# Gates and mix_out of a decoder layer in pairs of column blocks, with seven block products for half of the depth, and the head's later loads moved behind its splits

## The chip, the core and the metric

The kernel runs on one core of one Trainium2 chip. The metric is the device time of one execution in microseconds (us). Most executions of one kernel agree within 0.3%.

## The reference

One decoder layer on 256 tokens of width 2048, all in float32. What matters here:

```python
h = rms_norm(x, norm_mix)
q, k, v, cx, cb, cc, ga, gc = split_in_proj(h @ w_in)
...
y_attn = merge_heads(moba_attention(q, k, heads(v, N_ATTN_HEADS))) @ w_attn_out
y_conv = (cb * short_conv(cc * cx, conv_w)) @ w_conv_out
merged = jax.nn.sigmoid(ga) * y_attn + jax.nn.sigmoid(gc) * y_conv
x = x + merged @ w_mix_out
hq = heads(rms_norm(x, norm_xattn) @ wq_x, N_XATTN_HEADS)
mk, mv = jnp.split(rms_norm(mem, norm_mem) @ wkv_x, 2, axis=-1)
...
u = jax.nn.relu(rms_norm(x, norm_mlp) @ w_up)
return x + (u * u) @ w_down
```

`w_in` is 2048 x 10240: 1024 columns each for q, k, v, cx, cb and cc, and 2048 each for the two gates ga and gc. `w_attn_out` and `w_conv_out` are 1024 x 2048, `w_mix_out` 2048 x 2048, `w_up` 2048 x 8192, `w_down` 8192 x 2048.

## The kernel before, in words

**Products.** A float32 operand is written as the sum of a high and a low part of type float32r, and a product is three matmuls: high by high, high by low, low by high (L103 to L105). TensorE (PE) multiplies a stationary 128x128 piece of the activations by 128 rows x 512 columns of the weights and adds into a PSUM bank.

**Weights.** They are streamed from HBM in raw tiles of 128x2x512 (two blocks of 128 rows, 512 KB) by SP's DMA queue (`load_w`, L58). ScalarE (ACT) rounds a tile to its high part (`whi`, L66), VectorE (DVE) subtracts to get the low part (`wlo`, L67); each is one instruction of 128x1024. The pool of raw tiles has 6 buffers, the pool of split ones 5 of each kind.

**Column groups.** `tok_group` (L107) makes 512 output columns for all 256 tokens: two PSUM banks, one for each 128 tokens, and for each block of 128 rows three matmuls of 512 columns a bank. A group 2048 deep is 96 matmuls and eight weight tiles. `feat_group`, used for w_up, gives the output transposed.

**Stages, in order of the program.** The head: w_in's first 512 columns, while x's features are still being loaded (`xf` into `xraw`, with the weights, on SP's queue) and split (`split_scaled`, L134/L135). x by tokens (`xtok`, 2 MB in four DMAs on ACT's queue, L246) is loaded in the same stretch, and its sums of squares (L189) are made on ACT; from them comes r1, the RMS factor that is multiplied in when a group is taken out of PSUM (L204). Then q, k, v; attention; the convolution's three groups and its elementwise part `y` (L318 to L321); then the loop over four column blocks j (L329): two groups of w_in for the gates with the sigmoid read from PSUM on ACT (L333), attn_out (L337), conv_out (L341, L342) and eight transposes that turn the merged block into features (`mg`). Then `residual` for mix_out: four groups, each added to xtok (L355) and transposed into `x2g` (L134/L135), with `memory(j)` after each: a load of mem by features (L372, ACT's queue) into a buffer of the pool `blk` (3 buffers), split into `memT`, and a load of mem by tokens (L376) for its sums of squares. Then cross attention and the MLP.

**Order.** The Tile framework places each engine's instructions by its own timeline, so they stand in another order than the program writes them; each engine and queue then runs its own list in order. Where an instruction needs a buffer, it waits until the buffer's last reader is done.

## Time and profile before

| what | value |
|---|---|
| median of 3 runs | 1476.53 us (1476.36 to 1476.88) |
| the profiled execution: its own time | 1476.77 us |
| its span, first to last instruction | 1475.0 us |
| mean granted TensorE clock | 0.996 of full speed |
| PE busy | 1454.8 us, 99% of the span |
| DVE busy | 820.9 us, 56% |
| ACT busy | 691.2 us, 47% |
| DMA | 281.27 MB, 191 GB/s on average |

Busy times are sums over instructions of the time between the start and the end that the profiler gives; on DVE and ACT an instruction that waits for nothing can start before the end of the one before it. The profile's 40 slices show PE at 9 tenths or more in all but the first slice (6). The execution's own time is 1.8 us more than its span, for what lies before the first and after the last instruction.

### The profile page before, as it was taken

The numbers are of one execution on the slowest core, as the hardware profiler recorded it, in microseconds if no ns is written. First come the engines' busy times: TensorE is split into PE (matmuls) and PEld (weight loads), VectorE is DVE, ScalarE is ACT, GpSimd is POOL, SyncE is SP. The second block draws the span as 40 slices with busy tenths as digits, with TensorE's granted clock in tenths as the row PEclk, the third lists the DMA queues.
The fourth block names the chain that finished last, engine by engine and source line by source line (L and its number), as shares of the span: only waits on it lengthen the run. The fifth ranks groups of instructions, "written<-read, shape, count | busy, mean of one in ns | idle before, by whom it ended". The sixth has DMA issues, their size and how long they took to land.

```text
span 1475.0 us, 18233 instructions
## 1 busy us (share of the span) xinstructions
PE 1454.8 (99%) x7064; PEld 1222.4 (83%) x7064; DVE 820.9 (56%) x976; ACT 691.2 (47%) x905; POOL 13.6 (1%) x21
## 2 busy tenths in 40 slices
PE   6999999999999999999999999999999999999997
PEld 5888888888888888888888888888888888888886
DVE  5545555765554646654476655556545555556554
ACT  6444544454444445554564443444434443445442
POOL 0000000000000000000000000000000000000011
PEclk9999999999999999999999999999999999999999
DMA  9666655576666667655555566565565556665652
GB/s 337 193 193 180 184 165 178 170 227 190 187 196 188 186 197 230 212 192 180 172 171 185 187 198 191 182 197 180 194 200 179 193 188 191 192 191 179 198 189 85
DMA packets 145158, 281.27 MB, mean 191 GB/s; under 512 B 8880, under 2 KB 9520, under 8 KB 144944
## 3 DMA queue, kind: packets, MB, share of 16 engines
q1 hardware_dynamic: 141888, 272.66, 58.9%
q10 hardware_dynamic: 3184, 7.45, 1.5%
q8 instruction: 55, 0.90, 0.2%
q14 instruction: 31, 0.25, 0.1%
HBM read 277.98 MB, written 2.10 MB: 190 GB/s over the span
## 4 chain that ended last, share of the span: by engine, by line
PE 98%; DMA 1%; ACT 1%; issue 0%; DVE 0%; POOLq 0%; POOL 0%; DVEq 0%; SPq 0%; ACTq 0%
PE acc L104 23%; PE acc L105 23%; PE acc L103 23%; PE acc L78 15%; PE acc L79 8%; PE aps L145 1%; PE acc L82 1%; DMA tok<-in_x_dram 1%; PE acc L81 1%; DMA raw<-in_w_in_dram 0%; ACT junk L189 0%; PE aps L315 0%; PE aps L270 0%; PE aps L438 0%; PE aps L407 0%
## 5 line engine op out<-in xcount | busy, mean ns | idle before, releaser
L67 DVE TENSOR_TENSOR wlo<-raw,whi 128x1024 fp32r<-128x1024 f32 (+1 forms) x510 | 618.7, 1222 | 561.2 <-ACT whi L66 547.5
L66 ACT ACTIVATE whi<-raw 128x1024 fp32r<-128x1024 f32 (+1 forms) x510 | 532.9, 1055 | 564.1 <-PE acc L105 386.2
L103 PE MATMUL acc<-whi,S 128*128 128x512 f32 x1512 | 584.9, 388 | 11.4 <-ACT whi L66 11.4
L105 PE MATMUL acc<-whi,S 128*128 128x512 f32 x1512 | 587.9, 389 | 0.0
L104 PE MATMUL acc<-wlo,S 128*128 128x512 f32 x1512 | 586.3, 388 | 0.3 <-DVE wlo L67 0.3
L103 PEld LDWEIGHTS acc<-whi,S 128*128 128x128 f32 x1512 | 284.6, 188 | 68.8 <-ACT whi L66 12.7
L78 PE MATMUL acc<-S,whi 128*128 128x512 f32 x960 | 341.6, 398 | 0.0
L104 PEld LDWEIGHTS acc<-wlo,S 128*128 128x128 f32 x1512 | 284.5, 188 | 58.8 <-DVE wlo L67 1.6
L105 PEld LDWEIGHTS acc<-whi,S 128*128 128x128 f32 x1512 | 284.7, 188 | 56.2
L79 PE MATMUL acc<-S,wlo 128*128 128x256 f32 x960 | 269.7, 281 | 0.0
L78 PEld LDWEIGHTS acc<-S,whi 128*128 128x128 f32 x960 | 180.4, 188 | 41.3
L79 PEld LDWEIGHTS acc<-S,wlo 128*128 128x128 f32 x960 | 181.3, 189 | 3.1
L474 ACT ACTIVATE blk<-acc 128x256 f32<-128x256 f32 x64 | 24.3, 380 | 36.0 <-PE acc L82 35.8
L189 ACT ACTIVATE junk<-tok 128x512 f32<-128x512 f32 (+1 forms) x33 | 20.2, 613 | 37.7 <-DVE tok L459 23.6
L459 DVE SCALAR_TENSOR_TENSOR tok<-acc,q,tok 128x512 f32<-128x512 f32 (+1 forms) x33 | 24.1, 731 | 18.0 <-PE acc L105 18.0
L130 ACT ACTIVATE S<-blk 128x512 fp32r<-128x512 f32 x32 | 20.0, 626 | 25.7 <-DVE blk L478 25.7
L475 DVE TENSOR_TENSOR blk<-acc,blk 128x256 f32<-128x256 f32 x64 | 27.0, 422 | 8.0 <-ACT blk L474 8.0
L131 DVE TENSOR_TENSOR S<-blk,S 128x512 fp32r<-128x512 f32 x32 | 22.1, 692 | 9.9 <-ACT S L130 8.4
L82 PE MATMUL acc<-S,whi 128*128 128x512 f32 x64 | 25.6, 400 | 0.0
L478 DVE SCALAR_TENSOR_TENSOR blk<-blk 128x512 f32<-128x512 f32 x32 | 22.0, 689 | 0.6
L204 ACT ACTIVATE blk<-acc,r 128x512 f32<-128x512 f32 x18 | 12.4, 689 | 15.5 <-PE acc L105 15.5
L81 PE MATMUL acc<-S,wlo 128*128 128x256 f32 x64 | 18.1, 283 | 0.0
(127 smaller groups left out, 466.2 us busy)
## 6 DMA issues: line engine op xcount, KB each, us to landing
raw<-in_w_in_dram SPq DMA_DIRECT2D x158, 512.0 KB, 4.2
raw<-in_w_up_dram SPq DMA_DIRECT2D x128, 512.0 KB, 4.0
raw<-in_w_down_dram SPq DMA_DIRECT2D x128, 512.0 KB, 4.3
raw<-in_w_mix_out_dram SPq DMA_DIRECT2D x32, 512.0 KB, 4.9
raw<-in_w_attn_out_dram SPq DMA_DIRECT2D x16, 512.0 KB, 4.3
raw<-in_w_conv_out_dram SPq DMA_DIRECT2D x16, 512.0 KB, 4.5
raw<-in_wkv_x_dram SPq DMA_DIRECT2D x16, 512.0 KB, 4.2
raw<-in_wq_x_dram SPq DMA_DIRECT2D x8, 512.0 KB, 3.9
```

What stands on the lines that cost most here:

```text
L66: nc.scalar.activation(hi[:, k:k + step, :], raw[:, k:k + step, :], AF.Copy)
L67: nc.vector.tensor_sub(lo[:, k:k + step, :], raw[:, k:k + step, :], hi[:, k:k + step, :].bitcast(F32))
L78: nc.tensor.matmul(ps, a, xs(k, 2), start=(k == 0), stop=False)
L79: nc.tensor.matmul(ps[:, S:], c, xs(k, 0), start=False, stop=False)
L81: nc.tensor.matmul(ps[:, S:], c, xs(k, 0), start=False, stop=False)
L82: nc.tensor.matmul(ps, a, xs(k, 2), start=(k == 0), stop=True)
L103: nc.tensor.matmul(ps, xh, wh, start=(k == 0), stop=False)
L104: nc.tensor.matmul(ps, xh, wl, start=False, stop=False)
L105: nc.tensor.matmul(ps, xl, wh, start=False, stop=(k == nk - 1))
L459: nc.vector.scalar_tensor_tensor(t, ps, q3[:, h:h + 1], t, op0=ALU.mult, op1=ALU.add)
L474: nc.scalar.activation(z[:, b, :], ps[:, S:], AF.Copy)
L475: nc.vector.tensor_add(z[:, b, :], ps[:, :S], z[:, b, :])
```

## The change

**Gates and mix_out by pairs of column blocks.** `pair_group` takes 1024 columns at once. A weight tile is now one block of 128 rows by 1024 columns (`load_row`, L124 of the new file). Two blocks of rows and two halves of the columns make a 2x2 matrix of weight blocks; two halves of the tokens and the two blocks of rows a 2x2 matrix of activation blocks. A pair of row blocks is multiplied in one of two ways:

- *plain*: eight block products, 24 matmuls, into four banks (q = 2, 3, 4, 8);
- *seven*: Strassen's seven products (in Winograd's form), 21 matmuls, into seven banks. For it DVE makes four sums of weight blocks, 128x512 each (`weight_sums`, L138 to L141), and five weight operands of 512 columns or more are split: one alone (`split_one`, L130/L131) and three tiles of 128x1024 (L70/L71), where a plain pair has two tiles. The sums of activation blocks are made once (`hsums`, `act_sums`, L149 to L152, split by L229/L230).

Of the eight pairs of a group four are seven and four plain, in the order of the tables `MIXED` and `MIXED_HIGH`. There are six such groups (two gates by two column pairs, and mix_out's two). After the last pair ACT copies one bank (L200), DVE makes four sums of banks (L201 to L204) in three buffers of `blk`, and each of the four outputs is a bank plus one of these (L442 for the gates, with the sigmoid behind it from SBUF; L480 and L481 for mix_out). A group uses all eight PSUM banks (pool mm 5 to 6, aux 3 to 2).

**Buffers.** Raw tiles 6 to 4, split tiles 5 to 4, new pools for the single split and the sums, and a few temporaries share tags. The gates' block `sg` (1024 columns now) takes xtok's memory, and xtok is loaded again before mix_out by one DMA of 2 MB on SP's queue (L472).

**The head.** The loads of xtok and of the rope table, and the sums of squares, are put behind the last split of the first group.

```diff
-    wraw = ctx.enter_context(tc.tile_pool(name="wraw", bufs=6))
-    wsp = ctx.enter_context(tc.tile_pool(name="wsp", bufs=5))
+    wraw = ctx.enter_context(tc.tile_pool(name="wraw", bufs=4))
+    wsp = ctx.enter_context(tc.tile_pool(name="wsp", bufs=4))
...
+    def weight_sums(r1_, r2_):
+        ta = wsum.tile([P, 2, 512], F32, name="tsum")
+        tb = wsum.tile([P, 2, 512], F32, name="tsum")
+        nc.vector.tensor_sub(ta[:, 0, :], r1_[:, 1, :], r1_[:, 0, :])
+        nc.vector.tensor_sub(ta[:, 1, :], r2_[:, 1, :], r1_[:, 1, :])
+        nc.vector.tensor_sub(tb[:, 0, :], r2_[:, 1, :], ta[:, 0, :])
+        nc.vector.tensor_sub(tb[:, 1, :], r2_[:, 0, :], tb[:, 0, :])
...
+        for pair, seven in order:
+            k = 2 * pair
+            r = [load_row(w, kr0 + k + i, c0) for i in range(2)]
...
+            if seven:
+                ta, tb = weight_sums(*r)
+                b11 = split_one(r[0][:, 0, :])
+                b21, b22 = split_w(r[1])
+                t1, t3 = split_w(ta)
+                t2, t4 = split_w(tb)
...
+                for q, a, b in ((1, act(0, 0), b11), (2, act(1, 0), b21), (3, s4, b22), (5, s1, t1), (7, s3, t3),
+                                (6, s2, t2), (4, act(1, 1), t4)):
+                    add(q, pair, a, b, True, True)
+            else:
+                b = [split_w(t) for t in r]
+                for q, h, j in ((2, 0, 0), (3, 0, 1), (4, 1, 0), (8, 1, 1)):
+                    for i in range(2):
+                        add(q, pair, act(i, h), b[i][j], i == 0, i == 1)
+        x, y, z = block(), block(), block()
...
+        nc.scalar.activation(p1, bank[1], AF.Copy)
+        nc.vector.tensor_add(u2, bank[6], p1)
+        nc.vector.tensor_add(u3, bank[7], u2)
+        nc.vector.tensor_add(u4, bank[5], u2)
+        nc.vector.tensor_add(v, bank[5], u3)
+        for q, h, j, u in ((2, 0, 0, p1), (3, 0, 1, u4), (4, 1, 0, u3), (8, 1, 1, v)):
+            evac(h, j, bank[q], u)
+    MIXED = [(0, True), (1, True), (4, False), (2, True), (5, False), (3, True), (6, False), (7, False)]
+    MIXED_HIGH = [((p + 4) % 8, s) for p, s in MIXED]
...
-                    if q >= 4:
-                        o = (q - 4) * 512
-                        nc.scalar.dma_start(xtok[:, :, o:o + 512], xv[:, :, o:o + 512])
-                nc.scalar.dma_start(csb, rope)
                 sp = const.tile([P, 2, 4], F32, name="r1sp")
-                for h in range(2):
+                with tc.issue_after(last_split[0].ins):
+                    nc.scalar.dma_start(csb, rope)
                     for d in range(4):
-                        sumsq(sp[:, h, d:d + 1], xtok[:, h, d * 512:(d + 1) * 512], 512)
+                        nc.scalar.dma_start(xtok[:, :, d * 512:(d + 1) * 512], xv[:, :, d * 512:(d + 1) * 512])
+                    for d in range(4):
+                        for h in range(2):
+                            sumsq(sp[:, h, d:d + 1], xtok[:, h, d * 512:(d + 1) * 512], 512)
+                hsums()
...
+    xtok = big.tile([P, 2, D], F32, name="tok")
+    nc.sync.dma_start(xtok, xv)
...
-    sp2 = residual(w_mix_out, KD, parts_of(mg), x2g, 1, "r2", memory)
+    sp2 = residual_pairs(w_mix_out, parts_of(mg), mS, x2g, 1, "r2", memory)
```

Three places in the engines' lists. First ACT at the head; `S` is here the split features of x, `tok` is xtok, `raw` and `whi` are a weight tile and its high part. Before:

```order
4 L246 DMA tok<-in_x_dram 128x2x512 x2
5 L134 ACTIVATE S_84<-S_85,gcol 128x256
6 L66 ACTIVATE whi<-raw 128x512
7 L246 DMA tok<-in_x_dram 128x2x512 x2
8 L247 DMA csb<-in_rope_dram 128x128
9 L134 ACTIVATE S_84<-S_85,gcol 128x256
10 L189 ACTIVATE junk,r1sp<-tok 128x512 x2
11 L66 ACTIVATE whi<-raw 128x512
12 L189 ACTIVATE junk,r1sp<-tok 128x512
13 L134 ACTIVATE S_84<-S_85,gcol 128x256
14 L189 ACTIVATE junk,r1sp<-tok 128x512 x3
15 L66 ACTIVATE whi<-raw 128x512
```

After the change, from the end of the first group's splits:

```order
18 L233 ACTIVATE S_90<-S_91,gcol 128x256 x4
19 L70 ACTIVATE whi<-raw 128x1024
20 L233 ACTIVATE S_90<-S_91,gcol 128x256 x2
21 L70 ACTIVATE whi<-raw 128x1024 x2
22 L352 DMA csb<-in_rope_dram 128x128
23 L354 DMA tok<-in_x_dram 128x2x512 x4
24 L70 ACTIVATE whi<-raw 128x1024 x2
25 L288 ACTIVATE junk,r1sp<-tok 128x512 x2
26 L70 ACTIVATE whi<-raw 128x1024
27 L288 ACTIVATE junk,r1sp<-tok 128x512 x4
```

The sums of squares that stood between the second and the third split now stand behind all of the first group's.

Second, SP's queue at the start of mix_out, after the change (before it held `L58 DMA raw<-in_w_mix_out_dram` 32 times in a row):

```order
28 L60 DMA raw<-in_w_conv_out_dram 128x2x512 x4
29 L124 DMA raw<-in_w_mix_out_dram 128x1024 x7
30 L472 DMA tok<-in_x_dram 128x2x2048
31 L124 DMA raw<-in_w_mix_out_dram 128x1024 x25
32 L60 DMA raw<-in_wkv_x_dram 128x2x512 x8
```

The reload of xtok stands ahead of the eighth weight tile.

Third, the boundary between mix_out's two groups after the change. On ACT (`blk` is a buffer of the pool of 3, `tsum` a tile of weight sums, `ohi` the single split):

```order
249 L70 ACTIVATE whi<-raw 128x1024 x3
250 L130 ACTIVATE ohi<-raw 128x512
251 L70 ACTIVATE whi<-raw 128x1024
252 L516 DMA blk<-in_memf_dram 128x1024
253 L70 ACTIVATE whi<-tsum 128x1024
254 L233 ACTIVATE S_4534<-blk,gcol 128x256 x4
255 L520 DMA blk<-in_mem_dram 128x2x512
256 L130 ACTIVATE ohi<-raw 128x512
257 L516 DMA blk<-in_memf_dram 128x1024
258 L288 ACTIVATE junk,r2sp<-tok 128x512
259 L233 ACTIVATE S_4534<-blk,gcol 128x256 x4
```

and on DVE, in the same place:

```order
498 L140 TENSOR_TENSOR tsum<-raw,tsum 128x512
499 L480 TENSOR_TENSOR tok<-blk,tok 128x512
500 L71 TENSOR_TENSOR wlo<-tsum,whi 128x1024
501 L481 TENSOR_TENSOR tok<-acc,tok 128x512
502 L234 SCALAR_TENSOR_TENSOR S_4534<-blk,gcol,S_4534 128x256
503 L481 TENSOR_TENSOR tok<-aps,tok 128x512
504 L234 SCALAR_TENSOR_TENSOR S_4534<-blk,gcol,S_4534 128x256 x2
505 L481 TENSOR_TENSOR tok<-acc,tok 128x512
506 L234 SCALAR_TENSOR_TENSOR S_4534<-blk,gcol,S_4534 128x256
```

The loads of mem, which before had a buffer of `blk` free during all of mix_out, now stand behind the evacuation of the first group, and the splits of mem among the next group's weight splits.

## Rows read from the trace of the kernel before

**Rows 1.** The page, parts 1 and 5: busy time by engine; costliest PE groups with idle time.

```profile
PE 1454.8 (99%) x7064; PEld 1222.4 (83%) x7064; DVE 820.9 (56%) x976; ACT 691.2 (47%) x905; POOL 13.6 (1%) x21
...
L103 PE MATMUL acc<-whi,S 128*128 128x512 f32 x1512 | 584.9, 388 | 11.4 <-ACT whi L66 11.4
L105 PE MATMUL acc<-whi,S 128*128 128x512 f32 x1512 | 587.9, 389 | 0.0
L104 PE MATMUL acc<-wlo,S 128*128 128x512 f32 x1512 | 586.3, 388 | 0.3 <-DVE wlo L67 0.3
```

**Rows 2.** Waits: engine, what waited for what, us in all, times, longest.

```profile
DVE wlo L67 <- ACT whi L66: 547.5, 273, 5.0
ACT whi L66 <- PE acc L105: 386.2, 287, 3.3
```

**Rows 3.** Timeline of DVE in the loop over j: start, duration, what, idle before.

```profile
397.04 2.59 DVE L67 TENSOR_TENSOR wlo<-raw,whi 128x1024 fp32r<-128x1024 f32 x2 [2.85 <-ACT whi L66]
402.48 2.59 DVE L67 TENSOR_TENSOR wlo<-raw,whi 128x1024 fp32r<-128x1024 f32 x2 [2.85 <-ACT whi L66]
...
427.23 0.69 DVE L341 TENSOR_TENSOR R<-acc,R 128x512 f32<-128x512 f32 x1 [0.40 <-PE acc L105]
427.96 0.69 DVE L342 TENSOR_TENSOR R<-R 128x512 f32<-128x512 f32 x1
```

**Rows 4.** Lines by form: groups with busy time, mean ns of one, idle time before.

```profile
L67 DVE TENSOR_TENSOR wlo<-raw,whi 128x1024 fp32r<-128x1024 f32 x506 | 616.0, 1226 | 555.3 <-ACT whi L66 541.5
L66 ACT ACTIVATE whi<-raw 128x1024 fp32r<-128x1024 f32 x506 | 530.5, 1058 | 563.0 <-PE acc L105 386.2 <-issue 131.5 <-PE acc L78 41.4
L337 DVE TENSOR_TENSOR R<-acc,R 128x512 f32<-128x512 f32 x8 | 5.5, 687 | 1.6 <-PE acc L105 1.6
L318 DVE TENSOR_SCALAR y<-aps,gcol 128x256 f32<-128x256 f32 x8 | 3.7, 479 | 3.6 <-PE aps L315 3.6
```

**Rows 5.** Timeline of DVE around the start of mix_out.

```profile
568.79 2.35 DVE L67 TENSOR_TENSOR wlo<-raw,whi 128x1024 fp32r<-128x1024 f32 x2
571.79 1.29 DVE L131 TENSOR_TENSOR S<-aps,S 128x512 fp32r<-128x512 f32 x2 [0.64 <-ACT S L130]
574.33 1.69 DVE L135 SCALAR_TENSOR_TENSOR S<-blk,gcol,S 128x256 fp32r<-128x256 f32 x4 [1.26 <-ACT S L134]
```

**Rows 6.** Timeline of PE at the head, to the last gap.

```profile
5.88 1.22 PE L103 MATMUL acc<-whi,S 128*128 128x512 f32 x2 [5.88 <-ACT whi L66]
...
10.99 0.73 PE L103 MATMUL acc<-whi,S 128*128 128x512 f32 x2 [2.18 <-ACT whi L66]
...
16.40 1.22 PE L103 MATMUL acc<-whi,S 128*128 128x512 f32 x2 [3.37 <-ACT whi L66]
17.41 0.63 PE L104 MATMUL acc<-wlo,S 128*128 128x512 f32 x1
17.84 0.63 PE L105 MATMUL acc<-whi,S 128*128 128x512 f32 x1
...
21.55 0.50 PE L104 MATMUL acc<-wlo,S 128*128 128x512 f32 x1 [0.26 <-DVE wlo L67]
```

**Rows 7.** The chain of waits at the head: start, us, what.

```profile
5.66 8.14 DMA tok<-in_x_dram
13.88 1.95 ACT junk L189 x6
...
16.75 1.22 ACT junk L189 x4
```

**Rows 8.** Windows: busy us of PE, PEld, DVE, ACT, POOL; granted clock, DMA share, GB/s.

```profile
14.00:18.00 4.00, 1.60 (x4) 1.28 (x5) 1.09 (x2) 4.00 (x13) 0.00 (x0) 0.50 1.03 353
...
20.00:36.00 16.00, 15.74 (x69) 12.67 (x68) 14.37 (x20) 13.21 (x20) 0.00 (x0) 1.00 1.03 379
36.00:100.00 64.00, 64.00 (x292) 53.05 (x290) 31.05 (x39) 29.88 (x34) 0.00 (x0) 1.00 0.65 198
571.00:663.00 92.00, 92.00 (x425) 76.20 (x423) 55.71 (x71) 54.68 (x90) 1.39 (x2) 1.00 0.66 213
```

**Rows 9.** DMA issues: KB each, median us from issue to landing.

```profile
raw<-in_w_mix_out_dram SPq DMA_DIRECT2D x32, 512.0 KB, 4.9
...
blk<-in_memf_dram ACTq DMA_DIRECT2D x4, 512.0 KB, 5.5
```

**Rows 10.** Timeline of ACT at the start of mix_out.

```profile
568.90 0.34 ACTq L372 DMA_DIRECT2D blk<-in_memf_dram  x1
...
573.79 1.71 ACT L134 ACTIVATE S<-blk,gcol 128x256 fp32r<-128x256 f32 x4 [1.55 <-DMA blk<-in_memf_dram]
```

More of the change, by code (lines that the diff above doesn't have):

```diff
@@ L65, in split_w @@
         for k in range(0, nk, step):
-            nc.scalar.activation(hi[:, k:k + step, :], raw[:, k:k + step, :], AF.Copy)
+            last_split[0] = nc.scalar.activation(hi[:, k:k + step, :], raw[:, k:k + step, :], AF.Copy)
             nc.vector.tensor_sub(lo[:, k:k + step, :], raw[:, k:k + step, :], hi[:, k:k + step, :].bitcast(F32))
@@ L116, in parts_of, with block @@
+    MIXED = [(0, True), (1, True), (4, False), (2, True), (5, False), (3, True), (6, False), (7, False)]
+    MIXED_HIGH = [((p + 4) % 8, s) for p, s in MIXED]
+    def block():
+        return blk.tile([P, 2, 512], F32, name="blk")
     def parts_of(t, k0=0):
@@ L124, in small @@
     def small(name, shape=(P, S), bufs=2):
-        return tmp.tile(list(shape), F32, name=name, tag=name, bufs=bufs)
+        tag = {"s": "ta", "xsum": "ta", "pT": "tb", "zm": "tb", "rsw": "tc", "y": "tc", "junk": "ta"}.get(name, name)
+        return tmp.tile(list(shape), F32, name=name, tag=tag, bufs=bufs)
     def split_act(dst, k, src, nk=1):
@@ L208, in hybrid_block, with hsums @@
     vtok = qkv[:, 4 * AW:].rearrange("p (h f) -> p h f", h=2)
-    def block():
-        return blk.tile([P, 2, 512], F32, name="blk")
+    hS = big.tile([P, 4, 2, 512], F32R, name="SS")
+    def hsums():
+        for pair in range(4):
+            z = block()[:, 0, :].rearrange("p (k s) -> p k s", k=2)
+            for i in range(2):
+                k = 2 * pair + i
+                nc.vector.tensor_scalar(z[:, i, :], xraw[:, k, :], g_of(0, k), None, op0=ALU.mult)
+            act_sums(hS, pair, z)
     def rotate(qk, h):
@@ new lines, in hybrid_block, with residual_pairs, ev, ev_f @@
+    xtok = big.tile([P, 2, D], F32, name="tok")
+    nc.sync.dma_start(xtok, xv)
+    def residual_pairs(w, xs, xsum, dst, gi, name, between):
+        sp = const.tile([P, 2, 4], F32, name=name + "sp")
+        for jp in range(2):
+            def ev(h, j, ps, u, jp=jp):
+                c = 2 * jp + j
+                t = xtok[:, h, c * 512:(c + 1) * 512]
+                nc.vector.tensor_add(t, u, t)
+                nc.vector.tensor_add(t, ps, t)
+                sumsq(sp[:, h, c:c + 1], t, 512)
+            def ev_f(b, pt, jp=jp):
+                for i in range(2):
+                    k = 8 * jp + b + i
+                    split_scaled(dst, k, pt[:, i * S:(i + 1) * S], g_of(gi, k))
+            pair_group(w, jp * 1024, 0, KD, xs, xsum, MIXED_HIGH, ev)
+            to_features(xtok, 8 * jp, 8, ev_f)
+            between(2 * jp)
+            between(2 * jp + 1)
+        return sp
```

94 lines of the change are left out of this document (77 added, 17 removed).

## The prediction

> **What bounds the kernel now.** First the page: PE is busy 99% of the span, and its costliest groups were idle 11.4 + 0.3 us in all [rows 1]. So time can come only from fewer or shorter matmuls, or from those 11.7 us, and any new wait of PE is paid in full. Next the waits: DVE's low split waits for ACT's high split, and ACT waits for the PE matmul that frees a buffer [rows 2]; both are early and held back by full buffers. Then the cadence: in the loop over j two tiles are split every 402.48 − 397.04 = 5.44 us [rows 3], which is what PE needs for two tiles of 12 matmuls: 0.2267 us for one of 512 columns. So the stages that change have the limit PE, and DVE has room: it needs two low splits in 5.44 us.
>
> How much room is a question of how DVE's time is read. The grouped lines give 1226 ns for a split of 128x1024, 1058 for ACT's, 687 for a 128x512 sum from PSUM, 479 for a 128x256 step [rows 4]. But where nothing holds DVE, one starts before the end of the last: two splits in 2.35 us, so 2.35 − 1.22 = 1.13 from start to start; two of 128x512 in 1.29 with 0.69 each, so 0.60; four of 128x256 in 1.69, so 0.40 [rows 5]. I call these paced times and take 1.14, 0.60 and 0.40.
>
> **The change part by part.** All sums are made against the profiled execution: 1476.77 us, of which 1475.0 is the span; the median of the runs, 1476.53, is 0.24 less.
>
> *Matmuls removed.* Six groups with four seven pairs each, three matmuls saved by each: 6 × 4 × 3 = 72, by 0.2267 us: **−16.3 us**. All lie on the path. Transposes and everything else on PE stay.
>
> *The head.* PE's gaps there are 2.18, 3.37 and 0.26 us after a start at 5.88 [rows 6]. The chain shows why: ACT waits in order for the xtok loads to 13.8 us and then sums squares, 1.95 and 1.22 us, with the next weight split behind them [rows 7]. The change puts both behind the splits. In the window 14 to 18 us the granted clock is 0.50, the lower of its two levels (1.2 GHz), after the 3.37 us gap [rows 8], and matmuls start 0.43 us apart [rows 6]; six of them so cost 6 × (0.43 − 0.227) = 1.2 us, which goes with the gap. Gaps 5.8 + clock 1.2 = 7.0. Bounds: 5 if the second block still waits some 0.5 us for x's features and the third too, 8.4 if the start and the third gap's low clock come out better as well. What could be late next: the sums of squares, now after all splits, and so r1, POOL's power step with it; but the first group's PSUM is emptied at some 37 us now, and PE has the next group's 96 matmuls in between, 22 us. DMA, at 379 GB/s from 20 to 36 us [rows 8], can bring the 2 MB later. **−7.0 us**.
>
> *Work added to DVE.* The lists show 1218 instructions for 978: per seven pair four sums of 128x512, one single split and one tile more; per group four sums of banks and the sums at the outputs. A seven pair costs DVE 4 × 0.60 + 0.60 + 3 × 1.14 = 6.4 us paced while PE takes 21 × 0.2267 = 4.8; a plain pair 2.3 against 5.4. Four of each with eight sums at the end: 4 × 6.4 + 4 × 2.3 + 8 × 0.60 = 39.6 us of DVE for 180 matmuls, 40.8 us. ACT has 4 × (0.6 + 3 × 1.06) + 4 × 2.12 = 23.6 us, no limit. So a group alone just fits, DVE at 97%. What doesn't fit is what stands among the groups, and is covered only by the lead of the splits: with four buffers three tiles of 2.72 us may stand ready, less one ACT and one DVE instruction (1.06 + 1.14), **6.0 us of lead at most**. Where DVE's list holds more than PE's work plus this lead, PE waits:
>
> - *First pair of gate groups.* The convolution's 32 elementwise steps and 8 splits now stand among the first three seven pairs: 40 × 0.40 = 16 us extra before the group's plain pairs come. From the group's first single split to its fourth, DVE's list holds 28.3 us at paced times and PE's 83 matmuls, 18.8 us: a fall of 9.5, less the lead of 6.0. **+3.5** (0 to 8: nothing if the convolution's steps lie early, 8 at the full durations of rows 4).
> - *Second pair of gate groups:* counted in the same way a fall of 4.4 to 5.0, under the lead: **+0.5** (0 to 3).
> - *From the gates to mix_out.* The activation sums of the last features hang on the transposes, and the 2 MB reload stands on SP ahead of the eighth mix_out tile and waits until the last transposes have read the shared buffer. At 379 GB/s [rows 8] it takes 5.5 us, then a tile lands 4.9 us later [rows 9]; four raw tiles of lead cover most. **+2.8** (0 to 8).
> - *Between mix_out's two groups.* DVE has eight sums (4.8), 16 scaled splits (6.4) and two seven pairs together; from the last split ahead of the sums to that of the second plain tile its list holds 28.3 us, PE's 62 matmuls, 14.1: a fall of 14.2 against a lead of 6.0, 8 us. ACT is worse placed: before, mem's load was issued at 568.90 and its split began at 573.79 [rows 10], at an idle `blk`; now the load waits for the buffers of the first group's sums, lands 5.5 us later [rows 9], and the weight splits stand behind, twice. Two waits of about 4.5 us with 5 us of other work between, less the lead, make 8 to 9 us; they fall partly together with DVE's. **+11.5** with 1 us for matmuls at the lower clock after a long gap (3 to 20: 3 if ACT's waits fall where DVE is behind anyhow and DVE runs faster, 20 if both add).
> - *Behind mix_out and elsewhere:* mem's second half behind the second group, and the smaller pools under w_up and w_down, where ACT and DVE are busy only 29.9 and 31.1 of 64 us in a quiet stretch [rows 8]: a tile ready takes 1.06 + 1.14 us and PE frees one in 2.72. **+1** (0 to 4). The other additions to ACT and DVE lie in DVE's free time: in mix_out's stretch before, 55.71 of 92 us were busy [rows 8].
>
> Sum: −16.3 − 7.0 + 3.5 + 0.5 + 2.8 + 11.5 + 1.0 = −4.0, so 1476.77 − 4.0 = 1472.8, as a median **1472.5 us**.
>
> **The rivals.**
>
> *A, the forecast:* half of the saving or more is given back as PE waits at the stage boundaries, most between mix_out's groups. Own range 1468 to 1478. Chance 0.40.
>
> *B, DVE and ACT keep up.* Waits of ACT and DVE lie inside each other, the lead hides the rest, and only some 8 us of waits stay: 1476.5 − 23.3 + 8 = 1461. For it: the paced times, and that DVE's and ACT's waits of before, 547.5 and 386.2 us [rows 2], are room. [...] Chance 0.25; 1459 to 1468.
>
> *C, slower: DVE keeps to its full durations.* In the seven pairs the four sums of weights partly read each other, and in the trace of before a sum that reads the last one's output started 427.96 − 427.23 = 0.73 us after it, not 0.60 [rows 3]. If that holds for all, a group costs DVE 4 × (5 × 0.69 + 3 × 1.23) + 4 × 2.45 + 8 × 0.69 = 43.9 us against PE's 40.8, and six groups cost 18 us more, less the lead where it stands (6 us): 12 above A, **1484**. It decides from 41 us of DVE a group on. The Trainium skill says as much (VectorE: DVE Perf Modes, "The DRAIN you can't avoid": the next operation does not start until the pipe is empty), and adds that one that is not held starts earlier; by the first half alone the time would be 1484, and the trace, with 1.13 us from start to start for splits of 1.22, is on the side of the second for independent ones. Against C: the lists put other work between most dependent sums. Chance 0.20; 1480 to 1490.
>
> *D, the head or the pools miss:* the head's gain stays away because x's features were late as well, or four buffers are too few under w_up, where the lead was five tiles. Then A plus 7: 1479.5, range 1476 to 1483. Chance 0.15.
>
> **How the numbers follow.** What a measurement can tell from no change is about 0.2%, 2.95 us: faster is below 1473.6, slower above 1479.5. Of A some 60% lies below 1473.6 and nearly all of the rest in between (0.24 and 0.15); B is faster (0.25); C slower (0.20); D half the same, half slower (0.07 and 0.08). So faster 0.50, same 0.22, slower 0.28. The range leaves out the lower half of B and the upper half of C: 1461 to 1483.
>
> **What would show it.** Right: 4440 matmuls of 512 columns at 0.227 us; at the head no gap over 1 us after the first matmul and granted clock 1.00 by 14 us; PE waits of some 10 us between mix_out's groups, with ACT's scaled splits waiting there for mem's DMA; DVE busy without gaps in the gate groups, its splits 1.13 us apart when in a row. Wrong: PE waiting inside every group with DVE never idle (C), PE waits of under 9 us in all (B), waits under w_up or w_down, or a gap at the head that stays (D).

## The result and the profile after

| | us |
|---|---|
| before, median | 1476.68 (1476.36 to 1476.88) |
| changed, median | 1486.39 (1486.06 to 1487.01) |
| ratio | 1.0066, 95% interval 1.0049 to 1.0084 |
| predicted | 1472.5, range 1461 to 1483 |

The change makes the kernel slower by 9.7 us. The page of the changed kernel, parts 1 and 5; compare [rows 1].

```profile
span 1484.3 us, 18431 instructions
...
PE 1450.6 (98%) x6992; PEld 1207.7 (81%) x6992; DVE 956.4 (64%) x1216; ACT 734.2 (49%) x971; POOL 17.7 (1%) x21
...
L108 PE MATMUL acc<-wlo,S 128*128 128x512 f32 (+1 forms) x1128 | 434.9, 388 | 2.1 <-DVE wlo L71 2.1
L107 PE MATMUL acc<-whi,S 128*128 128x512 f32 (+1 forms) x1128 | 429.4, 388 | 5.9 <-ACT whi L70 5.9
```

The 72 matmuls are gone (6992 instructions for 7064), but the span grew by 9.3 us. PE's busy time can't say where, because a matmul's end is modelled and a late start is partly hidden in it. So I take the starts: over all of PE's timeline, the time from one matmul's start to the next, less what the step takes when nothing waits (0.227 us after 512 columns, 0.120 after 256, 0.109 after a transpose), the late first start counted in. The sums of that excess by stretch, in us, for eleven kernels of this study (times from the span's start; the kernels' stages lie at nearly the same times; matmuls at the lower clock count in with what they take over 0.227 us):

```
              head   36 to  280 to 340 to 475 to 555 to 600 to 640 to
              to 36     60     340    365    505    600    640    760
before        15.8     0.0     0.2    0.0    0.0    0.1    0.1    3.4
after          9.4     3.1     8.6    2.3    2.3    3.9   12.4    4.7
e2 gates       9.5     3.4     8.5    2.4    2.1    0.1    0.1    4.0
e3 mix         8.2     0.5     0.1    0.0    0.0    1.5   12.6    5.5
e4 mem early   8.7     1.7     9.2    2.5    2.3    9.4    7.6    4.0
e5 raw 6       9.8     0.0     6.1    1.2    0.4    5.2   10.4    5.7
e6 plain 1st   8.8     0.0    12.7    5.7    2.6    4.1   14.2    5.0
e8 plain 1st   8.4     0.0    10.0    5.5    0.2    0.1    0.1    4.0
e9 gates, 6    8.4     0.0     5.8    1.2    0.3    0.1    0.1    4.0
e11 mem        8.8     0.0     7.4    1.2    0.1    3.4    6.5    7.8
e13            9.2     0.0     0.2    0.2    0.0    0.1    0.1    4.0
```

The stretches are: the head; q and k; the first gate group; its end and the next group's start; the start of the second pair of gate groups; gates to mix_out; between mix_out's groups; mix_out's end and cross attention. Each row is one execution, whose time lies up to 1.9 us from its kernel's median (e5; above it). Of the stretches left out two changed: 365 to 475 us by +0.4, and from 760 us on by −1.9. The whole sum rose from 29.0 to 54.7 us, by 25.7; less the 72 × 0.227 = 16.3 us of matmuls this gives +9.4, within 0.1 us of the change of the span.

The same stretches as windows of the changed kernel; compare [rows 8].

```profile
36.00:60.00 24.00, 22.27 (x98) 16.98 (x97) 18.32 (x47) 16.98 (x27) 5.01 (x1) 1.00 0.63 199
...
280.00:340.00 60.00, 54.87 (x239) 43.25 (x238) 54.31 (x82) 31.30 (x38) 0.00 (x0) 0.97 0.51 158
...
475.00:505.00 30.00, 29.04 (x124) 22.54 (x123) 26.95 (x32) 19.08 (x23) 0.00 (x0) 1.00 0.57 188
555.00:600.00 45.00, 43.26 (x187) 33.75 (x186) 42.60 (x59) 26.00 (x32) 0.00 (x0) 1.00 0.64 222
600.00:640.00 40.00, 32.33 (x132) 23.91 (x131) 35.83 (x55) 25.83 (x49) 0.00 (x0) 0.91 0.59 194
```

In each of these stretches DVE is busy for 76 to 95% of the time, and from 60 to 280 us PE lost nothing new. At the head the gap of 3.37 us is gone (the longest after the first matmul is 0.89 us), and so is the low clock:

```profile
14.00:18.00 4.00, 3.48 (x14) 2.58 (x15) 3.98 (x6) 3.56 (x6) 0.00 (x0) 1.00 1.05 389
```

In the first gate group the forecast's count, from the first single split to the fourth, can be held against the timelines of DVE and PE:

```profile
281.61 0.68 DVE L131 TENSOR_TENSOR olo<-raw,ohi 128x512 fp32r<-128x512 f32 x1
311.21 0.69 DVE L131 TENSOR_TENSOR olo<-raw,ohi 128x512 fp32r<-128x512 f32 x1 [0.76 <-ACT ohi L130]
...
287.64 0.40 PE L169 MATMUL acc<-ohi,S 128*128 128x512 f32 x1
311.23 0.50 PE L169 MATMUL acc<-ohi,S 128*128 128x512 f32 x1 [1.60 <-ACT ohi L130]
313.94 0.77 PE L169 MATMUL aps<-whi,S 128*128 128x512 f32 x1 [1.25 <-DVE y L428]
```

DVE took 29.6 us from the first to the fourth, the first stood about 6 us ahead of the matmul that reads it, and PE had lost 4.9 us when it reached the fourth. The rest of the loss, 3.5 us, came behind that point, and 2.3 us more at the next group's start. The chain of waits of the changed kernel shows what held PE in the group: start, us, what.

```profile
304.57 0.60 DVE tsum L140
305.17 0.39 DVE y L426
305.57 1.14 DVE wlo L71
306.73 3.72 DMA raw<-in_w_in_dram
310.55 0.64 ACT ohi L130
311.21 0.69 DVE olo L131
311.90 0.78 DVE y L426 x2
312.69 0.78 DVE y L427 x2
313.46 0.34 DVE y L428
313.94 0.77 PE aps L169
```

DVE runs without a break to 306.7; then a weight row's load is on the path for 3.7 us from issue to landing, which no term of the forecast had. Behind it the convolution's last step (`y`, L428) lets PE go on into an `aps` bank: the pool of two PSUM banks that the transposes and two of the group's eight sums share. The waits say why the load is late: who waited for what, us, times, longest. By SP's queue, the three largest of L124:

```profile
SPq L124 <- DVE wlo L71: 130.7, 53, 10.8
...
SPq L124 <- DVE tsum L141: 51.2, 16, 8.9
SPq L124 <- DVE tsum L139: 42.8, 18, 5.2
```

and by ACT:

```profile
ACT S L233 <- DMA blk<-in_memf_dram: 12.9, 4, 4.4
...
ACT ohi L130 <- DMA raw<-in_w_in_dram: 11.4, 8, 3.3
```

SP can't issue a row's load (L124) before DVE has made the low split and, in a seven pair, the weight sums from the row that holds the buffer, and ACT's single split then waits for the landing. SP waits nearly as long with six raw buffers (e5: 54.6 and 41.7 us for the sums), so these sums of waits show the order of things and not what it costs PE; that is for the runs. The first of ACT's lines is mem's, as foreseen. DVE's own pace is in its timeline between mix_out's groups:

```profile
598.43 2.35 DVE L71 TENSOR_TENSOR wlo<-raw,whi 128x1024 fp32r<-128x1024 f32 x2
600.70 0.68 DVE L202 TENSOR_TENSOR blk<-acc,blk 128x512 f32<-128x512 f32 x1
601.30 0.68 DVE L203 TENSOR_TENSOR blk<-acc,blk 128x512 f32<-128x512 f32 x1
601.90 0.68 DVE L138 TENSOR_TENSOR tsum<-raw 128x512 f32<-128x512 f32 x1
602.50 0.68 DVE L131 TENSOR_TENSOR olo<-raw,ohi 128x512 fp32r<-128x512 f32 x1
```

Splits follow at 1.13 us and sums at 0.60, as in [rows 5].

And ACT in the same place:

```profile
602.37 1.06 ACT L70 ACTIVATE whi<-raw 128x1024 fp32r<-128x1024 f32 x1 [1.84 <-DMA raw<-in_w_mix_out_dram]
602.45 0.35 ACTq L516 DMA_DIRECT2D blk<-in_memf_dram  x1
603.90 1.06 ACT L70 ACTIVATE whi<-tsum 128x1024 fp32r<-128x1024 f32 x1 [0.47 <-DVE tsum L139]
608.25 0.51 ACT L233 ACTIVATE S<-blk,gcol 128x256 fp32r<-128x256 f32 x1 [3.28 <-DMA blk<-in_memf_dram]
...
614.20 0.51 ACT L233 ACTIVATE S<-blk,gcol 128x256 fp32r<-128x256 f32 x1 [3.11 <-DMA blk<-in_memf_dram]
...
617.39 1.04 ACT L70 ACTIVATE whi<-tsum 128x1024 fp32r<-128x1024 f32 x1
```

Between one split of weight sums (603.90) and the next (617.39) lie 13.5 us with mem's work and its two waits.

### The profile page after: what moved, and what is told of

Read it like the earlier page. It is cut to its first block, busy times and chain, and to the rows that moved or that the text cites. A ratio compares the mean times of both kernels' runs of the same rounds, so it can differ in the third digit from the quotient of the medians.

```text
span 1484.3 us, 18431 instructions
## 1 busy us (share of the span) xinstructions
PE 1450.6 (98%) x6992; PEld 1207.7 (81%) x6992; DVE 956.4 (64%) x1216; ACT 734.2 (49%) x971; POOL 17.7 (1%) x21
## 4 chain that ended last, share of the span: by engine, by line
PE 85%; DVE 6%; DMA 5%; ACT 2%; issue 1%; ACTq 0%; SPq 0%; POOLq 0%; POOL 0%; DVEq 0%
PE acc L107 16%; PE acc L108 16%; PE acc L109 16%; PE acc L82 15%; PE acc L83 8%; DVE wlo L71 3%; DMA raw<-in_w_in_dram 2%; PE acc L170 2%; PE acc L171 2%; PE acc L169 2%; DMA raw<-in_w_mix_out_dram 1%; PE aps L169 1%; PE aps L171 1%; PE aps L170 1%; PE acc L86 1%
## 5 line engine op out<-in xcount | busy, mean ns | idle before, releaser
L71 DVE TENSOR_TENSOR wlo<-raw,whi 128x1024 fp32r<-128x1024 f32 (+1 forms) x486 | 588.6, 1221 | 424.3 <-ACT whi L70 413.9
L70 ACT ACTIVATE whi<-raw 128x1024 fp32r<-128x1024 f32 (+1 forms) x486 | 504.8, 1053 | 479.1 <-PE acc L109 270.0
L108 PE MATMUL acc<-wlo,S 128*128 128x512 f32 (+1 forms) x1128 | 434.9, 388 | 2.1 <-DVE wlo L71 2.1
L107 PE MATMUL acc<-whi,S 128*128 128x512 f32 (+1 forms) x1128 | 429.4, 388 | 5.9 <-ACT whi L70 5.9
L109 PE MATMUL acc<-whi,S 128*128 128x512 f32 (+1 forms) x1128 | 434.1, 387 | 0.0
L107 PEld LDWEIGHTS acc<-whi,S 128*128 128x128 f32 x1128 | 212.0, 188 | 48.9 <-ACT whi L70 7.3
L108 PEld LDWEIGHTS acc<-wlo,S 128*128 128x128 f32 x1128 | 212.5, 188 | 46.3 <-DVE wlo L71 4.6
L109 PEld LDWEIGHTS acc<-whi,S 128*128 128x128 f32 x1128 | 212.4, 188 | 42.0
L70 ACT ACTIVATE whi<-tsum 128x1024 fp32r<-128x1024 f32 x48 | 50.7, 1058 | 39.9 <-DVE tsum L141 21.1
L71 DVE TENSOR_TENSOR wlo<-tsum,whi 128x1024 fp32r<-128x1024 f32 x48 | 58.3, 1219 | 4.5 <-ACT whi L70 4.0
L170 PE MATMUL acc<-wlo,S 128*128 128x512 f32 x120 | 47.6, 397 | 2.4 <-DVE wlo L71 2.4
L169 PE MATMUL aps<-whi,S 128*128 128x512 f32 x120 | 45.5, 398 | 2.3 <-DVE y L428 1.2
L170 PE MATMUL aps<-wlo,S 128*128 128x512 f32 x120 | 47.2, 394 | 0.0
L171 PE MATMUL aps<-whi,S 128*128 128x512 f32 x120 | 47.2, 394 | 0.0
L171 PE MATMUL acc<-whi,S 128*128 128x512 f32 x120 | 47.0, 392 | 0.0
L169 PE MATMUL acc<-whi,S 128*128 128x512 f32 x120 | 43.5, 398 | 0.8 <-ACT whi L70 0.8
```

Source lines behind the costliest of these rows:

```text
L70: last_split[0] = nc.scalar.activation(hi[:, k:k + step, :], raw[:, k:k + step, :], AF.Copy)
L71: nc.vector.tensor_sub(lo[:, k:k + step, :], raw[:, k:k + step, :], hi[:, k:k + step, :].bitcast(F32))
L107: nc.tensor.matmul(ps, xh, wh, start=(k == 0), stop=False)
L108: nc.tensor.matmul(ps, xh, wl, start=False, stop=False)
L109: nc.tensor.matmul(ps, xl, wh, start=False, stop=(k == nk - 1))
L169: nc.tensor.matmul(bank[q], ah, bh, start=first, stop=False)
```

## The experiments

Theory at the start: the loss is the sum of local losses, by place, as in the table. Rival: a shared limit (DVE, small pools), so that what is taken from one place comes back at another. All runs are compared with the kernel before, run on the same chip beside them (1476.55 to 1476.71 us).

**e1: the head alone, on the kernel before.**

```diff
-                    if q >= 4:
-                        nc.scalar.dma_start(xtok[:, :, o:o + 512], xv[:, :, o:o + 512])
-                nc.scalar.dma_start(csb, rope)
...
+                with tc.issue_after(last_split[0].ins):
```

> The kernel before with the head's change alone: the loads of xtok and of the rope table and the sums of squares stand behind the first group's splits; no pair groups, the pools as before. Theory: the two traces, each matmul's start compared with the one before it, put 15.8 us of late start and gaps before 36 us in the kernel before and 10.1 us in the changed one, so the head gives 5.7 us; the 2.4 us that PE loses at 40 to 51 us in the changed kernel come from the activation sums that DVE makes there for the gates, which this kernel lacks. Expected 1476.7 - 5.7 = 1471.0 us. Rival: the 2.4 us come from the late sums of squares and the late factor r1, so they stay: 1473.4 us. Second rival: the head gives nothing that lasts: 1476.7.

Measured 1470.29 us, ratio 0.9956 (0.9941 to 0.9971). The head is worth 6.3 us and nothing is given back at 36 to 60 us (0.1): in this kernel, with six raw buffers, the late r1 costs nothing.

**e2: the gates alone; e3: mix_out alone** (each with the head's change and the small pools).

```diff
-    sp2 = residual_pairs(w_mix_out, parts_of(mg), mS, x2g, 1, "r2", memory)
+    sp2 = residual(w_mix_out, KD, parts_of(mg), x2g, 1, "r2", memory)
```

> The changed kernel with mix_out's four groups as before (no seven products there, no activation sums for it); the head, the gates in pairs and the small pools stay. Theory: PE's losses add up by place. 48 matmuls fewer (10.9 us), head 5.7 less 2.4 given back, first pair of gate groups +10.5, second +2.4, the rest +0.5 to 2 for the reload of xtok: 1476.7 - 10.9 - 3.3 + 12.9 + 1 = 1476.4 us. Rival: what PE loses between mix_out's groups was caused by the small pools and comes back at another boundary: above 1480.

> The changed kernel with the gates as before (four column blocks, sigmoid from PSUM, their block in its own memory, so that xtok is never reloaded) and mix_out in pairs; no activation sums at the head. Theory: 24 matmuls fewer (5.4 us), head 5.7 (or 3.3), the step from the gates to mix_out +1 to 3.8, between mix_out's groups +12.4: 1476.7 - 5.4 - 5.7 + 2 + 12.4 = 1480.0 us. Rival: the losses between mix_out's groups come from DVE being late already from the gates, so that without these they halve: 1474.

Measured: e2 1473.89 (0.9981, 0.9972 to 0.9991), e3 1479.09 (1.0016, 1.0006 to 1.0025). Against the head alone the gates cost 3.6 us for 10.9 us of matmuls saved, mix_out 8.8 for 5.4. The losses mostly add up: 8.5 us at the first gate group and 12.6 between mix_out's groups stand at their places whether the other part is there or not, so DVE doesn't carry lateness from one into the other. The times add to 1482.7, 3.7 short of the change. 2.3 us of that stand from the gates to mix_out (3.9 in the change against 0.1 and 1.5), where only the change has both the reload of xtok (e3 has none) and a mix_out in pairs.

**e4: mem's work in the attn_out and conv_out groups of the second pair.**

```diff
             tok_group(w_attn_out, jp * 1024 + o, 0, 8, parts_of(acT), ev_a)
+            if jp == 1:
+                memory(2 * c)
...
```

> The changed kernel with mem's loads, scaled splits and sums of squares called in the second pair's attn_out and conv_out groups instead of behind mix_out's groups (memT and x2g change places in memory for it); the work is the same. Theory: between mix_out's groups PE loses 12.4 us because ACT waits twice for mem's loads (3.28 and 3.11 us) with the weight splits behind it and DVE has 16 scaled splits more; both go, some 4 to 5 us stay for the sums of banks and the transposed features, and the attn_out and conv_out groups have DVE time to spare: 1486.4 - 8 = 1478.4 us. Rival: DVE had no gap from 594.96 to 617.4 us, so the sums and the seven products alone keep PE waiting and mem's part only fills the gaps: 1485.

Measured 1487.06 (1.0069, 1.0054 to 1.0084). Between mix_out's groups the loss falls from 12.4 to 7.6 us, but from 505 to 600 us it rises from 3.9 to 11.1. Its windows:

```profile
555.00:600.00 45.00, 40.07 (x163) 30.06 (x162) 42.20 (x67) 27.53 (x40) 10.31 (x1) 0.96 0.58 200
600.00:640.00 40.00, 35.81 (x153) 26.26 (x152) 37.56 (x52) 24.00 (x37) 0.00 (x0) 1.00 0.51 170
```

So the rival was right in outcome (1485), for another reason: mem's part did cost between mix_out's groups, but it cost no less in the place it was moved to. DVE's load alone doesn't tell why: from 555 to 600 us it is busy 42.20 of 45 us, and 42.60 in the change. What e4's trace shows there is ACT's single split waiting for a row of mix_out (at most 1.7 us in the change), with weight splits behind it, and then a wait of PE; why the row is late stays open:

```profile
554.61 0.63 ACT L130 ACTIVATE ohi<-raw 128x512 fp32r<-128x512 f32 x1 [5.31 <-DMA raw<-in_w_mix_out_dram]
...
561.11 0.50 PE L108 MATMUL acc<-wlo,S 128*128 128x512 f32 x1 [2.91 <-DVE wlo L71]
```

**e5: six raw buffers.**

```diff
-    wraw = ctx.enter_context(tc.tile_pool(name="wraw", bufs=4))
+    wraw = ctx.enter_context(tc.tile_pool(name="wraw", bufs=6))
...
-    xo = big.tile([P, NX, 2, S], F32R, name="R")
+    xo = big.tile([P, NX, 2, S], F32R, name="SS")
```

> The changed kernel with six raw weight buffers instead of four (the cross attention's output takes the activation sums' memory to make room). Theory: a raw row stays in its buffer until DVE has made the weight sums and the low split from it, so with four buffers the next pair's load is issued only when DVE is through, and its landing comes after: 3.7 us at 306.7 and 3.6 us at 350.2 stand in the chain of the changed kernel as DMA, and ACT's single split waits 15.3 us in all for raw rows. With six, half to all of the loss at the first gate group (8.2), its end (2.3), the second pair (2.2) and the step to mix_out (3.8) goes: 1486.4 - 8 to 12, so 1476 us. Rival: DVE's list is what is full there, the raw rows are late only because DVE is, and DVE then takes the DMA's place in the chain: 1485.

Measured 1478.44 (1.0012, 1.0003 to 1.0022): 8.0 us less than the change. In the table the 3.1 us at 36 to 60 go altogether, 2.5 of the first gate group's 8.6, 1.1 of 2.3 at its end, 1.9 of 2.3 at 475, 2.0 between mix_out's groups. (With the same first gate group e11 loses 7.4 there and e9 5.8, and e4, with four buffers, 9.2: what the buffers are worth in the group is known to some 1.5 us.) Windows of e5, for the first and the third of the rows of after:

```profile
36.00:60.00 24.00, 24.00 (x112) 19.96 (x111) 18.79 (x49) 17.09 (x31) 5.00 (x1) 1.00 0.72 231
...
475.00:505.00 30.00, 29.96 (x132) 24.34 (x131) 27.13 (x31) 17.64 (x19) 0.00 (x0) 1.00 0.67 214
```

DVE does the same work in them and PE no longer waits: there it was not DVE's load. But at 36 to 60 us, where all tiles are plain, four buffers alone are not the cause either. Up to 47.48 us ACT waits 3.34 us for r1, POOL's power step (L296), with four weight splits behind it. The first line is POOL's and the next two ACT's in the changed kernel, the last is POOL's in e6, which also has four raw buffers:

```profile
42.44 5.01 POOL L296 TENSOR_TENSOR r<-r1ss,mhalf 128x2 f32<-128x2 f32 x1 [40.27 <-DVE r1ss L294]
47.48 1.27 ACT L303 ACTIVATE blk<-acc,r 128x512 f32<-128x512 f32 x2 [3.34 <-POOL r L296]
48.64 3.90 ACT L70 ACTIVATE whi<-raw 128x1024 fp32r<-128x1024 f32 x4
...
40.08 0.71 POOL L297 TENSOR_TENSOR r<-r1ss,mhalf 128x2 f32<-128x2 f32 x1 [37.92 <-DVE r1ss L295]
```

With four buffers and a step of 5.0 us PE loses 1.3 to 1.4 us from 46 to 60 us (the change, e2, e4), with four buffers and 0.71 us 0.1 or less (e3, e6), with six buffers and 5.0 us nothing (e5, e10 to e14). What makes the step 5.0 or 0.71 us long no run shows. The rest, before 46 us (1.7 us in the change, 0.0 to 0.4 in e3, e4 and e6), stands where ACT's sums of squares wait for the late xtok (1.29 and 1.37 us in the change) ahead of weight splits. A wait on the gates' way to mix_out stays (5.2).

**e6: plain pairs first in the first gate group.**

```diff
+    PLAIN_FIRST = [(4, False), (5, False), (6, False), (0, True), (1, True), (2, True), (3, True), (7, False)]
...
```

> The changed kernel with another order of pairs in the first gate group alone: three plain pairs first, then the four seven pairs, one plain pair last. Theory: PE loses 10.5 us in and behind that group because the convolution's 40 steps stand in DVE's list among the first seven pairs; beside plain pairs, where DVE has 2.3 us of splits in 5.4 us of PE, they are free, and four seven pairs in a row cost DVE 25.7 us against 19.0, which the lead of 6 us takes: 1486.4 - 7 = 1479. Rival: the four seven pairs in a row are over the lead with the group's end, and the loss only moves to the start of the second gate group: 1485.

A miss: 1494.19 us (1.012, 1.0102 to 1.0138), 7.8 more than the change. The chain of waits in this group:

```profile
297.65 3.65 DMA raw<-in_w_in_dram
...
331.04 5.07 DMA raw<-in_w_in_dram
336.13 0.64 ACT ohi L130
```

Raw rows are late twice, and PE's transposes of the convolution wait 3.05 us for an `aps` bank that the last `y` step frees. I had counted DVE's time and not when rows and banks come free. The number of buffers doesn't settle it: e8 has this order with six raw buffers and still loses 10.0 and 5.5 us here (e6 12.7 and 5.7), with rows' loads of 4.18, 4.73 and 6.07 us in its chain. Why this order makes the rows late stays open.

**e7: the small pools alone, on the kernel before.**

```diff
-    wraw = ctx.enter_context(tc.tile_pool(name="wraw", bufs=6))
-    wsp = ctx.enter_context(tc.tile_pool(name="wsp", bufs=5))
+    wraw = ctx.enter_context(tc.tile_pool(name="wraw", bufs=4))
+    wsp = ctx.enter_context(tc.tile_pool(name="wsp", bufs=4))
```

> The kernel before with four raw and four split buffers instead of six and five, nothing else. Theory: a plain tile needs 4.2 us of load and 2.2 us of splits against 2.72 us of PE a tile, so four buffers of each hold it; outside the head nothing is lost, and at the head the fifth and sixth early tile come later, which costs at most 1 us: 1476.7 to 1477.7. Rival: PE waits now and then under w_up and w_down: above 1480.

Measured 1475.14 (0.9989, 0.9979 to 0.9999), no slower: in the kernel before, four buffers are enough for plain tiles. So they come short with seven pairs, whose sums hold a raw row longer, and with plain tiles only where ACT's list stops, as at 36 to 60 us (e5).

**e8: gates alone, six raw buffers, plain pairs first, activation sums behind the first v group.**

```diff
...
+        if c == 0:
+            hsums()
...
```

> The gates in pairs with room: mix_out as before, six raw buffers, plain pairs first in the first gate group, and the activation sums for the gates made behind the first v group instead of at the head. Theory: from the kernel with the gates alone, 1473.9, goes 2.5 us at 40 to 51 us, 7 us at the first gate group and 3 us at the other starts of groups: 1462 us. Rival, by which DVE is simply full in the gate groups: 2.5 us go at the start, the rest moves: 1470.

A miss: 1474.67 (0.9987, 0.9978 to 0.9997). The order of e6 cost here too (10.0 and 5.5 us at 280 and 340, against 5.8 and 1.2 in e9). e9 takes it out:

**e9: gates alone with six raw buffers, the change's order.** (The edits of e2 and e5.)

> The kernel with the gates alone in pairs (mix_out as before), with six raw buffers in place of four; the order of pairs as in the change. Theory, the raw buffers: of what PE loses with the gates alone, 2.9 us at 40 to 60 us, 2.4 at 340, 2.0 at 480 and some 2 of the 8.3 at 300 go, as they did in the full kernel: 1473.9 - 7 to 8, so 1466.5 us, under the 1470.3 of the head alone. Rival: with mix_out plain the raw rows have time anyhow, and the step is worth 3 us or less: 1471.

Measured 1467.67 (0.9938, 0.9923 to 0.9953), as the theory had it: 6.2 us under e2 and 2.6 under the head alone. What is left at the first gate group, from PE's timeline:

```profile
304.33 0.50 PE L169 MATMUL acc<-ohi,S 128*128 128x512 f32 x1 [0.80 <-DVE y L428]
308.50 0.47 PE L169 MATMUL aps<-whi,S 128*128 128x512 f32 x1 [2.33 <-DVE y L428]
```

No raw row stands in its chain of waits any more, though ACT's single split still waits 4.73 us for one at 303.65; PE waits for the convolution's last steps.

**e10: only two late seven pairs in that group.**

```diff
+    FEW = [(4, False), (5, False), (0, True), (6, False), (2, False), (1, True), (7, False), (3, False)]
...
```

> As the run beside it (gates alone, six raw buffers), but in the first gate group only two pairs are seven, third and sixth in the order, so that the convolution's steps stand beside plain pairs. Six matmuls more (1.4 us). Theory: what six raw buffers leave at 290 to 320 us (6.0 us) is DVE's convolution steps between the seven pairs; with plain pairs there 5 us go: 1466.5 + 1.4 - 5 = 1463 us. Rival: it is the wait for the convolution's last low splits and transposes, whatever the pairs are: 1467.

A miss of the theory, 1470.58 (0.9958, 0.9943 to 0.9973): 7.2 us are lost at 280 to 340 us, more than in e9. PE's wait for `y` at the `aps` bank is 2.74 us, no shorter than with four seven pairs (2.33 in e9). A plain pair needs both `aps` banks within its 24 matmuls. The rival's reading, that the convolution's last steps set the time whatever the pairs are, fits, but its time (1467) was missed too.

**e11: six raw buffers and mem behind mix_out; e12: with e10's order as well.**

```diff
-    sp2 = residual_pairs(w_mix_out, parts_of(mg), mS, x2g, 1, "r2", memory)
+    sp2 = residual_pairs(w_mix_out, parts_of(mg), mS, x2g, 1, "r2", lambda j: None)
+    for j in range(4):
+        memory(j)
...
-    by_features(wkv_x, xm, rm, mkT)
     by_features(wq_x, parts_of(x2g), r2, hqT)
+    by_features(wkv_x, xm, rm, mkT)
```

> The changed kernel with six raw buffers (1478.4 us), and all of mem's loads, scaled splits and sums of squares behind mix_out's second group, with the query's group ahead of the keys' so that the features of mem have a plain group's time. Theory: between mix_out's groups PE loses 10.4 us, of which ACT's wait for mem's loads and DVE's 8 scaled splits of mem make 5; behind mix_out, with plain tiles, they cost 0 to 2: 1478.4 - 4 = 1474.5 us. Rival, by which DVE's sums of banks and seven pairs are enough: 3 us or less go there, and 2 to 4 come back behind mix_out: 1478.

> The changed kernel with six raw buffers, two late seven pairs in the first gate group, and mem behind mix_out: all three steps. Theory: they add up, 1474.5 + 1.4 - 5 = 1471 us, which is no better than the head alone (1470.3), because mix_out's pairs still cost more than their 5.4 us. Rival: DVE is a common limit and what is taken from one place comes back at the next: 1476.

Measured: e11 1476.51 (1.0001, 0.9991 to 1.001), e12 1477.24 (1.0008, 0.9997 to 1.0019). In e11's trace the loss between mix_out's groups falls from 10.4 to 6.5 us, so mem's part of it is about 4, and 2.1 us come back behind mix_out (7.8 for 5.7). The executions of e11 spread over 8 us, so its gain of 1.9 over e5 stands less firmly than its trace. e12's third step did nothing, as e10 would have it.

**e13: the first gate group as before, the other three in pairs, six raw buffers.**

```diff
+            if i == jp == 0:
+                for j in range(2):
...
+                    tok_group(w_in, 6 * AW + j * 512, 0, KD, hx, ev_0)
+                continue
```

> The gates alone with six raw buffers (1467.7 us), but the first gate group is made as before, as two groups of 512 columns with the sigmoid read from PSUM; three gate groups stay in pairs. 12 matmuls more, 2.7 us. Theory: that group lost 5.7 us at 280 to 320 us and 1.2 at its end, since the convolution's steps on DVE hold both PSUM banks of the pool of two that the group's products need, and share DVE with its weight sums; both go: 1467.7 + 2.7 - 6.5 = 1464 us. Rival: the group gives what it costs, as its 2.7 us are only half of the loss but the next group then starts beside late convolution steps: 1468.

Measured 1463.79 (0.9914, 0.9899 to 0.9928): the forecast of the theory, and the best kernel of the study, 12.8 us under the kernel before and 6.5 under the head alone. This group is made in banks of the other pool and has no weight sums, so the run takes both away at once. Its window (e9 lost 5.8 us there):

```profile
280.00:340.00 60.00, 60.00 (x276) 49.62 (x275) 42.52 (x60) 31.38 (x37) 0.00 (x0) 1.00 0.57 176
```

**e14: two of the convolution's three taps left out.** This kernel leaves 16 DVE steps of the convolution away.

```diff
-            nc.vector.scalar_tensor_tensor(y[:, 1:], pt[:, 0:S - 1], cw_of(1, f), y[:, 1:], op0=ALU.mult, op1=ALU.add)
-            nc.vector.scalar_tensor_tensor(y[:, 2:], pt[:, 0:S - 2], cw_of(0, f), y[:, 2:], op0=ALU.mult, op1=ALU.add)
```

> The gates alone with six raw buffers, with two of the convolution's three taps left out (two of four DVE steps a block, 16 in all, 6.4 us of DVE; the output is then not the reference's, the matmuls and loads are all there). Theory, DVE's list: PE's loss at 280 to 320 us, 5.7 us, falls to 1 or less, since the last steps end 6 us earlier and the PSUM banks with them: 1467.7 - 5 = 1462.7 us. Rival, by which the transposes and the bank handed on from one reader to the next set the time and not DVE's load: a loss of 4 or more stays, 1466.5.

Measured 1463.34 (0.9913, 0.9897 to 0.993), 4.3 us under e9; the loss at 280 to 340 us falls from 5.8 to 2.4. That lies between the theory (1 or less) and the rival (4 or more). So 3.4 us of it hang on these 16 steps. The run doesn't separate DVE's time from the time for which a bank is held, since the same steps do both, and no run gave the pool its third bank back.

**e15: mix_out's second group begun with plain pairs.**

```diff
+    LATER = [(0, False), (1, False), (4, True), (2, False), (5, True), (3, False), (6, True), (7, False)]
...
```

> The changed kernel with six raw buffers and mem behind mix_out (1476.5 us), and mix_out's second group begun with two plain pairs, with three seven pairs in it, no two in a row. Three matmuls more (0.7 us). Theory: the 6.5 us that stay between mix_out's groups come from two seven pairs in a row (12.8 us of DVE against 9.5 of PE) on top of DVE's eight sums and eight scaled splits; begun with plain pairs 4 us go: 1473 us. Rival: PE waits there for the end of the first group (the last outputs added, transposed and split) whatever follows: 1477.

A miss: 1484.28 (1.0057, 1.004 to 1.0075), 7.8 us over e11. Between the groups the loss falls only from 6.5 to 5.4, and 12.8 us stand behind mix_out (7.8 in e11). PE's waits between the groups:

```profile
609.51 1.06 PE L245 MATMUL aps<-ident,tok 128*128 128x128 f32 x8 [1.25 <-DVE S L235]
612.34 0.77 PE L169 MATMUL aps<-whi,S 128*128 128x512 f32 x1 [1.76 <-DVE S L235]
```

PE waits for the scaled splits of the transposed features, which free an `aps` bank: the rival's reading, the end of the first group (the lines of this kernel stand one further on, L234 and L244 of the change). Nor is the loss behind mix_out explained by the theory; there ACT waits 2.78 and 2.70 us for mem's loads and PE behind it 3.34 and 1.13 us, with the granted clock at 0.91 from 640 to 700 us (0.97 in e11).

## Why the prediction was wrong

- **Matmuls removed, −16.3:** right (72 fewer, spaced 0.227 us).
- **The head, −7.0:** right: −6.4 in the trace, −6.3 us in e1, with the gap and the low clock gone as said. That a late r1 costs nothing held in e1 and not in the change (next point).
- **"The other additions to ACT and DVE lie in DVE's free time":** wrong at 36 to 60 us, +3.1 where nothing was forecast. DVE had the time (18.32 of 24 us). The forecast asked of r1 only whether PE had other matmuls meanwhile, and not what stands behind it in ACT's list: ACT's waits for xtok and for r1 held up weight splits, and four raw buffers didn't cover that (e5: 0.0 with six).
- **First pair of gate groups, +3.5 (0 to 8):** this step failed most: 8.4 + 2.3 = +10.7, over its bound. As far as it was counted, to the fourth single split, the sum was near: 4.9 us lost for 3.5, with 29.6 us of DVE for 28.3 and a lead of about 6 us as taken (in part by luck, as 1.8 of the 4.9 are the wait at the fourth split, for the raw row). It failed in what it left out: it ended the count there and had DVE's list and the lead as the only limits. Behind that point PE waits for an `aps` bank that the convolution's last steps hold, and matmuls go at the lower clock after it (3.5 us), and the next group starts late (2.3 us, with a row's load of 3.56 us in the chain). The runs show two things in place of the one limit: raw rows whose loads are issued late, since their buffers are held by the sums and splits (3.6 of the 10.7 go with six buffers, e5), and the convolution's steps on DVE, which also hold the two `aps` banks (3.4 go with half of them, e14; nearly all goes with the pairs, e13). The change names both pools, from 6 to 4 and from 3 to 2, and I priced the first for plain tiles and as lead alone (right: e7 and the 6 us) and the second not at all.
- **Second pair, +0.5 (0 to 3):** +2.3; 1.9 of it goes with six raw buffers.
- **Gates to mix_out, +2.8 (0 to 8):** +3.8, by the mechanism named: SP issues the reload at 570.47 us and the eighth row behind it at 570.95, and this row's load stands in the chain for 8.38 us.
- **Between mix_out's groups, +11.5 (3 to 20):** +12.3, with mem's two waits for its loads (3.28 and 3.11 us) where they were expected and the granted clock at 0.91 in the window. The size is in part luck: ACT's two waits were put at 4.5 us each and their part at 8 to 9, and raw buffers weren't in the term. What remains open is the split among its causes: mem some 4 us of it (e11), raw buffers 2.0 (e5), the rest, 6.5, the group's own end (sums, transposes, scaled splits, banks), which e15 points to but does not take apart.
- **Behind mix_out and elsewhere, +1:** +1.3 to 760 us, and 1.9 less after it.

Together the waits came to 33.9 − 1.9 = 32.0 us against 19.3 forecast; the head and the matmuls gave what was said. Of the rivals, the time fell into C's range (1480 to 1490), and C was not its cause: DVE kept its paced 1.13 and 0.60 us in the full stretches. The rule that VectorE's next operation waits for the pipe to empty (the Trainium skill, VectorE: DVE Perf Modes, "The DRAIN you can't avoid") would space splits by their 1.22 us; the changed kernel's trace again has 1.13, on the side of its exception for operations that aren't held. B was wrong. D was wrong as put, since the head's gain came and nothing was lost under w_up and w_down (1.9 us less from 760 us on), though the small pools did cost elsewhere. A was right that the stage boundaries give the saving back, most between mix_out's groups, and wrong in having no term for late raw rows and held banks.

## What to carry to other kernels

A scheme that saves work on the full engine by giving it to others has to be priced for every pool it turns over, and not only for the engine's time: how long does each operand now stay in its buffer, and when can the next load be issued? Here six raw buffers instead of four, found in memory that was free at the time, were worth 8 us, where the reorderings that were tried lost time. Where the helper engine is already busy with another stage (the convolution, the end of a group), leave the old scheme there and take the saving only where PE doesn't wait: three of six groups in pairs, with the head's change and six raw buffers, gave 12.8 us, and all six with four buffers lost 9.7.
